# A two-layer mixer model on one core: the forgetting attention issued as one chain, its causal mask added by VectorE

## The chip, the cores and the metric

One core of one Trainium2 chip runs the whole program. The metric is device time in microseconds, the median of three runs. The engines are TensorE (PE, and PEld for its weight loads), VectorE (DVE), ScalarE (ACT), GpSimd (POOL) and SyncE (SP), which issues the weight transfers.

## The reference, cut to what matters

A first block of two layers (mixer and dense feed-forward, then mixer and mixture of experts) is followed by a second block. All 512 tokens are one sequence, the model width is 1024. Each mixer holds three branches, whose outputs are joined and multiplied by `w_out`: a gated delta rule, the forgetting attention (6 heads of 64) and a pooling branch. The attention is what changes:

```python
for i in range(T // FX_BLOCK):                 # blocks of 128 queries
    lo, hi = i * FX_BLOCK, (i + 1) * FX_BLOCK
    s = jnp.einsum('bhqd,bhkd->bhqk', q[:, :, lo:hi], k[:, :, :hi]).astype(F32) * scale
    s = s + c[:, :, lo:hi, None] - c[:, :, None, :hi]
    s = jnp.where(k_pos <= q_pos, s, -jnp.inf)
    p = jax.nn.softmax(s, axis=-1).astype(dt)
    outs.append(jnp.einsum('bhqk,bhkd->bhqd', p, v[:, :, :hi]))
```

There are 6 heads with 4 query blocks each, so 24 blocks per mixer; block i has 128(i+1) keys.

## The kernel before

`mixer` (it runs twice, for the layers 0 and 1) builds everything as Python generators, called fibers. `Fibers.run` is a planner: it keeps a virtual time, resumes the ready fiber with the best rank, adds a cost for each matmul, and so writes down one order of instructions for TensorE. `yield 3.0` means "not before 3 us from now", `yield on(...)` waits for an event that another fiber sets, and `yield "pf"` waits for a free PSUM bank of the kind `pf`, of which there are three. TensorE executes the written order as it stands (`manual_schedule`); each instruction still waits for its data by semaphores, and the planned waits themselves are not in the program. The other engines are ordered by the framework.

The fibers around the change, with their ranks (a lower one goes first):
- `scan` (0.2): the recurrence of the delta rule, eight chunks with six small matmuls or twelve at a time, banks `px`. When it ends, its result is normalised, transposed and gated (`dn`).
- `heads` (1): transposes queries and keys of a head into two `fF` tiles, through `pf` banks; a head waits for the last scores of the head two before it.
- `attend(k)` (2), three of them: fiber k handles the blocks k, k+3, k+6 and so on.
- `dense` (3): input projections, pooling and gate columns, then the output projection. This is in two halves of eight output tiles. The first needs the pooling branch and `fo[0]`, the attention's first two heads; the second waits for `fo[1]`, `fo[2]` (the last head pair) and `dn`. While a planned heat is low, `dense` and `attend` go ahead of the others.

A block u of `attend` (head h = u // 4, query block i = u % 4) waits for its head and for the scores of block u-1 to be issued, and takes a `pf` bank. TensorE multiplies queries by keys into it and then adds the mask with a second matmul, the identity times the mask, both in the single-pass format fp32r (`causal_r`, lines 1171 to 1177). VectorE takes the maximum (line 1087), ScalarE the exponential with its sum (1089), VectorE the reciprocal (1090) and the scaling (1091) into the tile `fP`. After a planned wait of 2.2 + 0.4(i+1) us TensorE transposes P back into the same bank and VectorE copies it out (1095); after another 0.7 + 0.12(i+1) us TensorE multiplies by the values, and ScalarE copies the result into `fo` (1101), after which the bank is free:

```python
yield 2.2 + 0.4 * (i + 1)
...
yield 0.7 + 0.12 * (i + 1)
...
act(fo[j][r, 128 * i:N], ps[r, 0:128], AF.Copy)
rel("pf", 0.5)
```

Of the kernel before, what the change touches and what calls it, by code (L numbers as in the profile page):

```python
# [11 lines left out]
F32R = mybir.dt.float32r  # L12
I32 = mybir.dt.int32
U32 = mybir.dt.uint32
AF = mybir.ActivationFunctionType
ALU = mybir.AluOpType
# [62 lines left out]
class Pack:  # L79
# [10 lines left out]
    def done(self):  # L90
        return np.ascontiguousarray(np.concatenate(self.cols, 1))
# [97 lines left out]
class Event:  # L189
    t = None  # L190


class Fibers:
# [17 lines left out]
    def rel(self, tag, lat=1.0):  # L211
        self.banks.setdefault(tag, []).append(self.t + lat)
# [72 lines left out]
class Net:  # L285
# [326 lines left out]
    def mixer(self, l, xd=None, moe=False):  # L612
        nc, A, L = self.nc, self.A, f"L{l}."
        F = self.F = self.pe.F = Fibers({"pm": 2, "pf": 3, "px": 3})
        on, done, rel = F.event, F.set, F.rel
# [15 lines left out]
        if xd is None:  # L631
            xd = self.spill_x()
        ident, bones, tri64 = self.const("ident"), self.const("bones"), self.const("tri64")
        g = {}
        cx = lambda a: a.rearrange("p (c x) -> p c x", c=8)
        tt, ts, stt, act = (nc.vector.tensor_tensor, nc.vector.tensor_scalar, nc.vector.scalar_tensor_tensor,
                            nc.scalar.activation)
# [12 lines left out]
        nc.vector.tensor_copy(fg[:, 1:2], self.p(L + "fk"))  # L650
        hon = self.sm("hon", 1)
        ts(hon, self.p(L + "on"), 0.5, None, op0=ALU.mult)
        idr, car = self.causal_r()
        tri_x = self.state_tri()
        kF, KB, Q, kT, qd = ([None] * 3 for _ in range(5))
        MQ = {}
# [2 lines left out]
        xt, fo, zs, py, dn = [None] * 3, [None] * 3, [], [], []  # L659
# [389 lines left out]
        fs = {}  # L1049

        def heads():
            yield on("U")
            for h in range(6):
                j, hh = h // 2, h % 2
                yield on("xt", j)
                if h > 1:
                    yield on("S", h - 2, 3)
                fs[h] = []
                for s in range(2):
                    yield "pf"  # L1060
                    ps = self.ps("pf")
                    for n in range(4):
                        self.pe.transpose(ps[0:65, 128 * n:128 * n + 128], xt[j][:, n, s, hh], ident)
                    f = self.t("fF", "g")
                    act(f[0:65], ps[0:65], AF.Copy, scale=fg[0:65, s:s + 1])
                    rel("pf", 0.9)
                    fs[h].append(f)
                done(0.9, "fs", h)

        def attend(k):  # L1070
            for u in range(k, 24, 3):
                h, i = u // 4, u % 4
                j, hh = h // 2, h % 2
                yield on("fs", h)
                if u:
                    yield on("S", (u - 1) // 4, (u - 1) % 4)
                if (hh, i) == (0, 0):
                    fo[j] = self.t("fo", "z")
                q, kk = fs[h]
                N = 128 * (i + 1)  # L1080
                yield "pf"
                ps = self.ps("pf")
                self.pe.matmul(ps[:, :N], q[0:65, 128 * i:N], kk[0:65, :N], start=True, stop=False)
                self.pe.matmul(ps[:, 128 * i:N], idr, car, start=False, stop=True)
                done(0.0, "S", h, i)
                nm = self.t("fnm", "fs", (128, 3), bufs=4)
                nc.vector.tensor_reduce(nm[:, 0:1], ps[:, :N], axis=AX, op=ALU.max, negate=True)
                P = self.t("fP", "q", (128, 2, T))[:, 0]
                act(P[:, :N], ps[:, :N], AF.Exp, bias=nm[:, 0:1], accum_out=nm[:, 1:2])
                nc.vector.reciprocal(nm[:, 2:3], nm[:, 1:2])  # L1090
                ts(P[:, :N], P[:, :N], nm[:, 2:3], None, op0=ALU.mult)
                yield 2.2 + 0.4 * (i + 1)
                for jj in range(i + 1):
                    self.pe.transpose(ps[:, 128 * jj:128 * jj + 128], P[:, 128 * jj:128 * jj + 128], ident)
                nc.vector.tensor_copy(P[:, :N], ps[:, :N])
                yield 0.7 + 0.12 * (i + 1)
                r = slice(64 * hh, 64 * hh + 64)
                for jj in range(i + 1):
                    self.pe.matmul(ps[r, 0:128], fv[:, jj, 64 * h:64 * h + 64],
                                   P[:, 128 * jj:128 * jj + 128], start=jj == 0, stop=jj == i)  # L1100
                act(fo[j][r, 128 * i:N], ps[r, 0:128], AF.Copy)
                rel("pf", 0.5)
                if (hh, i) == (1, 3):
                    done(0.5, "fo", j)

        for rank, gen in enumerate((rstd(), gates(), scan(), intra(), keys(), decay(), values())):
            F.add(gen, 0.1 * rank)
# [1 line left out]
            F.add(queries(j), 0.7)  # L1109
            F.add(qnorm(j), 0.8)  # L1110
        F.add(heads(), 1)
        for k in range(3):
            F.add(attend(k), 2)
        F.add(dense(), 3)
        if moe:
            F.add(self.dispatch(), 0.01)
# [50 lines left out]
        nc.gpsimd.tensor_scalar(y[:, 16:], s[:, 16:], pin, None, op0=ALU.mult)  # L1167
        nc.gpsimd.tensor_tensor(y, y, x, op=ALU.subtract)


    def causal_r(self):
        if not hasattr(self, "_cr"):
            t = self.M.tile([128, 2, 128], F32R, name="car", bufs=1)
            self.nc.vector.tensor_copy(t[:, 0], self.const("ident"))
            self.nc.vector.tensor_copy(t[:, 1], self.const("causal"))
            self._cr = (t[:, 0], t[:, 1])
        return self._cr

    def swiglu(self, f, pg, pu, R):
        nc = self.nc  # L1180
# [1195 lines left out]
```

## Time and profile before

| | us |
|---|---|
| median of 3 runs | 2715.37 (2712.01 to 2716.12) |
| profiled execution, its own time | 2711.52 |
| its span, first to last instruction | 2709.7 |
| TensorE busy in the span | 2582.4 (95%) |
| VectorE busy | 1578.1 (58%) |
| ScalarE busy | 1126.0 (42%) |
| mean granted TensorE clock | 0.977 |

The mixers' attention lies at 195.7 to 289.4 us and at 877.7 to 976.8 us of the span. The granted clock is a share of 2.4 GHz, so 0.50 is 1.2 GHz. In the rows an engine's busy time in a stretch can be subtracted from the length of the stretch to get its idle time. Rows of matmuls overlap, since they are pipelined; distances between starts tell what one costs in a stream.

### The profile page before, as it was taken

What the parts mean: (1) busy time and instruction counts of PE and PEld (TensorE: products, weight loads), DVE (VectorE), ACT (ScalarE), POOL (GpSimd) and SP (SyncE); (2) the same over time, 40 slices, a digit from 0 to 9 for tenths busy, and PEclk for the clock granted to TensorE, in tenths of its full rate; (3) what the DMA queues carried; (4) which work ended last, traced back from release to release, by engine and by line L of the source; (5) the groups of instructions that cost most, each with busy time, mean ns of one, the idle gap of its engine ahead of it and who ended that gap; (6) DMA issues with size and microseconds to landing.
All of it is one profiled execution on the core that took longest, in us unless ns stands there. A gap on an engine that the chain in (4) does not pass through costs nothing.

```text
span 2709.7 us, 44079 instructions
## 1 busy us (share of the span) xinstructions
PE 2582.4 (95%) x18168; PEld 2001.5 (74%) x18168; DVE 1578.1 (58%) x2269; ACT 1126.0 (42%) x1608; POOL 376.5 (14%) x295
## 2 busy tenths in 40 slices
PE   7999999999999999999999998899989999999997
PEld 6787788888778667777777776566666676788887
DVE  5856743434575655666766675566744644644445
ACT  4344432223434534555555555464323334433332
POOL 4332000000333301000000001143432000000000
PEclk9999999999999999999999999999999999999999
DMA  3111222222312226687777766413232522222221
GB/s 115 55 57 41 85 93 94 94 93 96 116 55 65 67 79 230 250 309 276 269 266 275 254 253 229 169 67 109 82 118 88 174 87 69 88 98 94 95 93 56
DMA packets 102610, 359.41 MB, mean 133 GB/s; under 512 B 12416, under 2 KB 17920, under 8 KB 102400
## 3 DMA queue, kind: packets, MB, share of 16 engines
q1 hardware_dynamic: 82656, 307.42, 33.1%
q0 software_dynamic: 7840, 26.22, 2.8%
q10 hardware_dynamic: 11904, 22.86, 2.3%
q8 instruction: 145, 2.38, 0.4%
q14 instruction: 65, 0.53, 0.1%
HBM read 331.28 MB, written 25.17 MB: 132 GB/s over the span
## 4 chain that ended last, share of the span: by engine, by line
PE 56%; DVE 7%; issue 3%; DMA 2%; ACT 2%; POOL 0%; ACTq 0%; DVEq 0%; POOLq 0%; SPq 0%
PE pm L278 34%; PE px L278 11%; PE pf L278 10%; PE px L282 1%; DVE ipr L477 1%; DVE cy L673 0%; DMA raw<-in_s_gu_dram 0%; DVE G L1583 0%; PE pf L282 0%; DVE wlo L398 0%; DMA ye<-y 0%; DVE Tl L478 0%; DMA yb<-ye,slot 0%; DMA ya<-ye,slot 0%; DVE wl L2029 0%
## 5 line engine op out<-in xcount | busy, mean ns | idle before, releaser
L396 ACT ACTIVATE whi<-raw 128x1024 fp32r<-128x1024 f32 (+5 forms) x304 | 297.6, 979 | 776.6 <-PE pm L278 519.5
L278 PE MATMUL pm<-xsh,whi 128*128 128x512 f32 x1280 | 530.7, 415 | 10.8 <-ACT xsh L371 5.0
L278 PE MATMUL pm<-xsl,whi 128*128 128x512 f32 x1280 | 511.5, 400 | 2.6 <-DVE xsl L372 2.6
L278 PE MATMUL pm<-xsh,wlo 128*128 128x512 f32 x1280 | 511.2, 399 | 2.7 <-POOL wlo L398 2.6
L2029 DVE TENSOR_TENSOR wl<-raw,wh 128x1536 fp32r<-128x1536 f32 (+1 forms) x224 | 341.4, 1528 | 190.2 <-PE pf L278 86.2
L2028 ACT ACTIVATE wh<-raw 128x1536 fp32r<-128x1536 f32 (+1 forms) x224 | 291.5, 1305 | 251.9 <-PE pf L278 127.7
L278 PEld LDWEIGHTS pm<-xsh,whi 128*128 128x128 f32 x1280 | 244.8, 191 | 87.9 <-issue 19.8
L278 PEld LDWEIGHTS pm<-xsl,whi 128*128 128x128 f32 x1280 | 244.8, 191 | 62.3 <-DVE xsl L372 6.1
L278 PEld LDWEIGHTS pm<-xsh,wlo 128*128 128x128 f32 x1280 | 243.9, 191 | 62.7 <-POOL wlo L398 5.0
L398 DVE TENSOR_TENSOR wlo<-raw,whi 128x1024 fp32r<-128x1024 f32 (+5 forms) x230 | 251.8, 1095 | 61.2 <-ACT whi L396 61.0
L398 POOL TENSOR_TENSOR wlo<-raw,whi 128x1024 fp32r<-128x1024 f32 x74 | 181.6, 2454 | 355.7 <-ACT whi L396 341.8
L278 PE MATMUL pm<-hidl,whi 128*128 128x512 f32 (+1 forms) x328 | 126.7, 386 | 0.0
L278 PE MATMUL pm<-hidh,wlo 128*128 128x512 f32 (+1 forms) x328 | 126.4, 385 | 0.0
L278 PE MATMUL pm<-hidh,whi 128*128 128x512 f32 (+1 forms) x328 | 125.9, 384 | 0.0
L278 PE MATMUL pf<-raw,xs 128*32 128x384 f32 x1024 | 102.5, 493 | 0.0
L278 PE MATMUL pm<-wh,xh 128*128 128x384 f32 x256 | 91.9, 370 | 8.0 <-ACT wh L2028 6.6
L1213 DVE TENSOR_TENSOR X<-X,pm 128x512 f32<-128x512 f32 x40 | 27.5, 687 | 120.2 <-PE pm L278 120.2
L278 PE MATMUL pm<-wl,xh 128*128 128x384 f32 x256 | 87.4, 342 | 2.9 <-DVE wl L2029 2.9
L278 PE MATMUL pm<-wh,xl 128*128 128x384 f32 x256 | 86.0, 336 | 0.0
L278 PE MATMUL pf<-wh,xl 128*128 128x384 f32 x256 | 85.8, 336 | 0.0
L278 PE MATMUL pf<-wl,xh 128*128 128x384 f32 x256 | 85.6, 335 | 0.0
L278 PE MATMUL pf<-wh,xh 128*128 128x384 f32 x256 | 84.4, 335 | 0.0
(625 smaller groups left out, 4805.2 us busy)
## 6 DMA issues: line engine op xcount, KB each, us to landing
raw<-in_s_gu_dram SPq DMA_DIRECT2D x128, 768.0 KB, 6.3
raw<-in_s_dn_dram SPq DMA_DIRECT2D x96, 512.0 KB, 4.0
raw<-in_f_gu_dram SPq DMA_DIRECT2D x44, 512.0 KB, 3.2
raw<-in_b_gu_dram SPq DMA_DIRECT2D x44, 512.0 KB, 3.2
raw<-in_b_wi_dram SPq DMA_DIRECT2D x38, 512.0 KB, 3.8
raw<-in_wq_dram SPq DMA_DIRECT2D x28, 512.0 KB, 3.5
raw<-in_f_dn_dram SPq DMA_DIRECT2D x16, 512.0 KB, 3.2
raw<-in_b_dn_dram SPq DMA_DIRECT2D x16, 512.0 KB, 3.2
```

The costliest lines, as they stand in the source:

```text
L278: return self.nc.tensor.matmul(o, l, r, **k)
L282: return self.nc.tensor.transpose(o, a, i)
L396: nc.scalar.activation(hi, raw, AF.Copy)
L398: (eng or nc.vector).tensor_tensor(lo, raw, hi.bitcast(F32), op=ALU.subtract)
L477: nc.vector.tensor_tensor(pr, A_, T_, op=ALU.mult)
L1213: nc.vector.tensor_tensor(self.X[m], self.X[m], ps, op=ALU.add)
L2028: self.wmark = act(hi, raw, AF.Copy)
L2029: tt(lo, raw, hi.bitcast(F32), op=ALU.subtract)
```

## The change

`attend` becomes one fiber with one loop over 26 steps. Step u issues the scores of block u, the values of block u-2 and the transposes of block u-1 together, with no planned wait between them, and one wait of 2.0 + 0.25(i+1) us at its end. The mask is added in PSUM by VectorE ahead of the maximum, and the fp32r copies of identity and mask are gone.

```diff
-        idr, car = self.causal_r()
...
-        def attend(k):
-            for u in range(k, 24, 3):
+        def attend():
+            blocks = {}
+            def scores(u):
                 h, i = u // 4, u % 4
-                yield on("fs", h)
-                if u:
-                    yield on("S", (u - 1) // 4, (u - 1) % 4)
...
-                yield "pf"
                 ps = self.ps("pf")
-                self.pe.matmul(ps[:, :N], q[0:65, 128 * i:N], kk[0:65, :N], start=True, stop=False)
-                self.pe.matmul(ps[:, 128 * i:N], idr, car, start=False, stop=True)
+                self.pe.matmul(ps[:, :N], q[0:65, 128 * i:N], kk[0:65, :N], start=True, stop=True)
                 done(0.0, "S", h, i)
                 nm = self.t("fnm", "fs", (128, 3), bufs=4)
+                tt(ps[:, 128 * i:N], ps[:, 128 * i:N], self.const("causal"), op=ALU.add)
                 nc.vector.tensor_reduce(nm[:, 0:1], ps[:, :N], axis=AX, op=ALU.max, negate=True)
...
-                yield 2.2 + 0.4 * (i + 1)
-                for jj in range(i + 1):
-                    self.pe.transpose(ps[:, 128 * jj:128 * jj + 128], P[:, 128 * jj:128 * jj + 128], ident)
-                nc.vector.tensor_copy(P[:, :N], ps[:, :N])
-                yield 0.7 + 0.12 * (i + 1)
+                blocks[u] = ps, P
+
+            def values_of(u):
+                ps, P = blocks.pop(u)
...
                 rel("pf", 0.5)
...
+            def turned(u):
+                ps, P = blocks[u]
+                N = 128 * (u % 4 + 1)
+                for j in range(0, N, 128):
+                    self.pe.transpose(ps[:, j:j + 128], P[:, j:j + 128], ident)
+                nc.vector.tensor_copy(P[:, :N], ps[:, :N])
+
+            for u in range(26):
+                if u < 24:
+                    yield on("fs", u // 4)
+                    yield "pf"
+                    scores(u)
+                if u > 1:
+                    values_of(u - 2)
+                if 0 < u < 25:
+                    turned(u - 1)
+                yield 2.0 + 0.25 * (u % 4 + 1) if u < 24 else 1.5
...
-        for k in range(3):
-            F.add(attend(k), 2)
+        F.add(attend(), 2)
```

## Rows read from the trace of the kernel before

**Rows 1.** The page: the span, and busy time of each engine.

```profile
span 2709.7 us, 44079 instructions
...
PE 2582.4 (95%) x18168; PEld 2001.5 (74%) x18168; DVE 1578.1 (58%) x2269; ACT 1126.0 (42%) x1608; POOL 376.5 (14%) x295
```

**Rows 2.** Table of stretches: length, busy us (instructions) by engine, granted clock, DMA share, GB/s.

```profile
195.70:302.60 106.90, 104.19 (x939) 77.84 (x938) 70.87 (x175) 49.44 (x125) 18.25 (x23) 0.98 0.13 42
289.40:302.60 13.20, 13.20 (x57) 10.66 (x58) 7.89 (x13) 4.15 (x8) 0.00 (x0) 1.00 0.33 96
...
877.70:990.10 112.40, 105.47 (x940) 78.08 (x939) 75.13 (x180) 54.42 (x137) 24.97 (x33) 0.97 0.20 63
...
976.80:990.10 13.30, 13.30 (x58) 10.79 (x59) 7.99 (x13) 4.15 (x8) 0.00 (x0) 1.00 0.34 96
```

**Rows 3.** TensorE in time order, first mixer: start, us, line, operation, x records.

```profile
226.59 0.65 PE L282 MATMUL pf<-cst,fP 128*128 128x128 f32 x4
227.08 0.39 PE L278 MATMUL pf<-fF 65*128 65x128 f32 x2
227.23 0.31 PE L278 MATMUL pf<-car 128*128 128x128 f32 x1
227.37 0.65 PE L278 MATMUL pf<-fF 65*128 65x256 f32 x2
...
228.20 0.39 PE L278 MATMUL pm<-xsl,whi 128*128 128x512 f32 x1
228.43 0.39 PE L278 MATMUL pm<-xsh,wlo 128*128 128x512 f32 x1
228.75 1.09 PE L278 MATMUL pf<-fP,fv 128*64 128x128 f32 x8
229.77 0.56 PE L278 MATMUL px<-Xc,Uf 64*64 64x64 f32 x12
```

**Rows 4.** TensorE's waits in both attentions: us in total, times, longest.

```profile
PE pf L278 <- ACT fo L1101: 1.1, 1, 1.1
PE px L278 <- ACT vn L994: 0.4, 1, 0.4
...
PE pf L278 <- ACT fo L1101: 2.2, 1, 2.2
PE pf L278 <- ACT fF L1065: 1.6, 1, 1.6
PE pf L278 <- DVE fP L1095: 0.8, 2, 0.6
PE pf L282 <- DVE fP L1091: 0.8, 1, 0.8
```

**Rows 5.** Stretches of 2 us, columns as in Rows 2: the clock behind stalls.

```profile
248.00:250.00 2.00, 0.97 (x3) 0.49 (x3) 2.00 (x4) 1.97 (x5) 0.00 (x0) 1.00 0.11 43
...
252.00:254.00 2.00, 2.00 (x7) 1.51 (x7) 0.88 (x3) 0.78 (x2) 0.00 (x0) 0.50 0.00 0
...
934.00:936.00 2.00, 0.00 (x0) 0.00 (x0) 1.97 (x6) 1.99 (x8) 0.77 (x2) 0.50 0.84 283
```

**Rows 6.** Softmax steps by tile (ns min/median/max), last: a PSUM addition (busy us, ns).

```profile
L1089 ACT ACTIVATE fP<-pf,fnm x48: 357/521/691, 198.0 to 970.8; 128x128 f32<-128x128 f32 x12, 128x256 f32<-128x256 f32 x12, 128x384 f32<-128x384 f32 x12, 128x512 f32<-128x512 f32 x12
L1089 ACT ACTIVATION_READ_ACCUMULATOR fP<-pf,fnm x48: 191/193/210, 198.3 to 971.3; 128x1 f32 x48
L1091 DVE TENSOR_SCALAR fP<-fP,fnm x48: 275/380/893, 199.3 to 972.9; 128x128 f32<-128x128 f32 x12, 128x256 f32<-128x256 f32 x12, 128x384 f32<-128x384 f32 x12, 128x512 f32<-128x512 f32 x12
L1095 DVE COPY fP<-pf x48: 269/481/685, 200.2 to 974.9; 128x128 f32<-128x128 f32 x12, 128x256 f32<-128x256 f32 x12, 128x384 f32<-128x384 f32 x12, 128x512 f32<-128x512 f32 x12
...
L1087 DVE TENSOR_REDUCE fnm<-pf x48: 278/484/692, 196.2 to 970.0; 128x1 f32<-128x128 f32 x12, 128x1 f32<-128x256 f32 x12, 128x1 f32<-128x384 f32 x12, 128x1 f32<-128x512 f32 x12
...
L1090 DVE RECIPROCAL fnm<-fnm x48: 144/156/164, 199.0 to 972.2; 128x1 f32<-128x1 f32 x48
...
L982 DVE TENSOR_TENSOR Xc<-px,nbe 128x192 f32<-128x192 f32 x7 | 2.5, 354 | 2.2 <-PE px L278 2.2
```

More of the change, by code (lines that the diff above doesn't have):

```diff
@@ L1068, in heads @@
                 done(0.9, "fs", h)
-        def attend(k):
-            for u in range(k, 24, 3):
+        def attend():
+            blocks = {}
+            def scores(u):
                 h, i = u // 4, u % 4
-                j, hh = h // 2, h % 2
-                yield on("fs", h)
-                if u:
-                    yield on("S", (u - 1) // 4, (u - 1) % 4)
-                if (hh, i) == (0, 0):
-                    fo[j] = self.t("fo", "z")
+                if u % 8 == 0:
+                    fo[h // 2] = self.t("fo", "z")
                 q, kk = fs[h]
                 N = 128 * (i + 1)
-                yield "pf"
                 ps = self.ps("pf")
-                self.pe.matmul(ps[:, :N], q[0:65, 128 * i:N], kk[0:65, :N], start=True, stop=False)
-                self.pe.matmul(ps[:, 128 * i:N], idr, car, start=False, stop=True)
+                self.pe.matmul(ps[:, :N], q[0:65, 128 * i:N], kk[0:65, :N], start=True, stop=True)
                 done(0.0, "S", h, i)
                 nm = self.t("fnm", "fs", (128, 3), bufs=4)
+                tt(ps[:, 128 * i:N], ps[:, 128 * i:N], self.const("causal"), op=ALU.add)
                 nc.vector.tensor_reduce(nm[:, 0:1], ps[:, :N], axis=AX, op=ALU.max, negate=True)
@@ L1091, in attend @@
                 ts(P[:, :N], P[:, :N], nm[:, 2:3], None, op0=ALU.mult)
-                yield 2.2 + 0.4 * (i + 1)
-                for jj in range(i + 1):
-                    self.pe.transpose(ps[:, 128 * jj:128 * jj + 128], P[:, 128 * jj:128 * jj + 128], ident)
-                nc.vector.tensor_copy(P[:, :N], ps[:, :N])
-                yield 0.7 + 0.12 * (i + 1)
-                r = slice(64 * hh, 64 * hh + 64)
+                blocks[u] = ps, P
+            def values_of(u):
+                h, i = u // 4, u % 4
+                ps, P = blocks.pop(u)
+                r = slice(64 * (h % 2), 64 * (h % 2) + 64)
                 for jj in range(i + 1):
@@ L1100, in attend @@
                                    P[:, 128 * jj:128 * jj + 128], start=jj == 0, stop=jj == i)
-                act(fo[j][r, 128 * i:N], ps[r, 0:128], AF.Copy)
+                act(fo[h // 2][r, 128 * i:128 * i + 128], ps[r, 0:128], AF.Copy)
                 rel("pf", 0.5)
-                if (hh, i) == (1, 3):
-                    done(0.5, "fo", j)
+                if u % 8 == 7:
+                    done(0.5, "fo", h // 2)
+            def turned(u):
[14 more added lines that the diff above has]
+                yield 2.0 + 0.25 * (u % 4 + 1) if u < 24 else 1.5
         for rank, gen in enumerate((rstd(), gates(), scan(), intra(), keys(), decay(), values())):
@@ L1168, in windows @@
         nc.gpsimd.tensor_tensor(y, y, x, op=ALU.subtract)
[L1171 to L1177, printed above, removed]
     def swiglu(self, f, pg, pu, R):
```

## The prediction, made before the result was known

> **What bounds the kernel now.** I read the page first, then a table of the stretches in which the attention of the two mixers runs, then the instructions of TensorE in order of time there, then what TensorE waited for, then the durations of the softmax steps. The page says that TensorE is the bound of the whole run: busy for 2582.4 of 2709.7 us [rows 1]. The change touches only two stretches. The first mixer's attention begins at 195.7 us, and its output projection has used up everything that does not need the last heads at 302.6; in the second mixer these points lie at 877.7 and 990.1 [rows 2]. In these stretches TensorE is idle for 106.90 - 104.19 = 2.7 us and 112.40 - 105.47 = 6.9 us. The mean granted clock is 0.98 and 0.97, so that up to 0.02 x 106.9 = 2.1 us and 0.03 x 112.4 = 3.4 us are lost to the lower level, 1.2 GHz. Take both away and each stretch holds 102.1 us of TensorE work at 2.4 GHz: the two agree to 0.1 us, as they should with the same list of instructions. So the stretch is TensorE work plus stalls, and the change can win only by removing work or stalls.
>
> One more pair of rows matters. From 289.4 (976.8), where the last block of attention has ended, to the end of the stretch TensorE is busy for 13.2 of 13.2 us (13.3 of 13.3) [rows 2]. This is projection work that needs only the first two heads. It covers the last block's softmax and the split of its result. Attention has so far a slack of 13 us.
>
> **Part 1: the mask leaves TensorE.** 48 matmuls (24 blocks, two mixers) of 128x128 against the identity go. Their rows are 0.3 us and more long, but matmuls overlap, so I take distances between starts. From the mask's start to the next start it is 0.14 us at the shortest [rows 3]; a matmul of 512 columns in the same number format follows its neighbour by 0.23 us, so 128 columns are 0.06 us. Between 48 x 0.06 = 2.8 and 48 x 0.14 = 6.7 us; I take 0.07, near the lower end, because the longer distance can hold the end of the scores' own stream: -3.4 us, 1.7 in each stretch. The Trainium skill (Perfetto Trace Analysis, Identifying the Most-Contended Engine) speaks against counting this: matmul busy time is no measure of how full TensorE is, weight-load time is. By that the 77.84 us of weight loads in 106.9 [rows 2] leave a quarter of it free and the term would be 0, the total 3.4 us higher; the trace agrees with the warning, since rows overlap, but the 0.23 us from start to start leaves no hole to fill.
>
> **Part 2: the mask comes to VectorE.** 48 additions of 128x128 from and to PSUM are not in the trace. The nearest rows are the evacuation of a 128x128 tile (0.27 us at least) and an addition of 128x192 with one operand in PSUM, 0.354 us [rows 6]; I take 0.29. That is 24 x 0.29 = 7.0 us on VectorE in each stretch, where it was busy for 70.87 of 106.9 us. It hides as long as blocks have slack. What is queued behind it on VectorE is the next scan step and the weight split, which TensorE waits for. Between 0 and 3 us in all; +1. The block's own latency from scores to probabilities becomes 0.29 + 0.48 (maximum) + 0.52 (exponential) + 0.19 (its sum) + 0.16 + 0.38 = 2.0 us by medians [rows 6]. The two casts at the start fall away with `causal_r`; they ran while the constants landed, 0.
>
> **Part 3: three interleaved chains become one.** This moves the most, in both directions.
>
> What it gives. Block u's transposes now stand a whole step behind its scores, its values another step behind that, and a PSUM bank is asked for a step after its eviction was issued instead of half a microsecond. The stalls of before are of just this kind: TensorE waited for the eviction `fo` (1.1 us in the first mixer, 2.2 in the second), for `fF` (1.6), for P's copy and scaling (0.8, 0.8) [rows 4]. Behind them the clock fell: 0.50 at 252 to 254 us after a stretch with 0.97 of 2 us busy, and 0.50 at 934 to 936, where nothing ran [rows 5]. Together there are 2.7 + 6.9 us idle and up to 2.1 + 3.4 us of clock, 15.1 us. Not all goes. The wait for `vn` is the scan's, and in the second mixer VectorE and ScalarE were both solid at 934 to 936 (1.97 and 1.99 of 2 us), so a backlog of some microseconds meets a slack of about two. Between 3 and 13 us; I take 60%, -9.
>
> What it costs. The order of TensorE is written by a planner, and the new chain waits 2.0 + 0.25(i+1) us after every step before the next may be issued. Over 24 blocks that is 24 x 2.0 + 0.25 x 60 + 1.5 = 64.5 us, one wait after another, where three chains used to wait side by side. The chain's own matmuls, from [rows 3]: per 128 columns of keys 0.23 us scores (0.29 less the mask), 0.49/4 = 0.12 transposes, 1.02/4 = 0.255 values, 0.61 x 60 = 36.5 us. The sum is 101.0 us against 102.1 - 1.7 = 100.4 us of all work that TensorE has there. So even if every step were picked up at once, the last block would be issued only when the covering work is gone; and it isn't picked up at once, for half a dense triple (0.35 us) is under way at the mean, more while the scan has the right of way: 24 x 0.35 = 8.4 us at least. So 9 us of planned waiting, 9/2.6 = 3.5 steps, have nothing beside them; I take 4, between 0 and 6. TensorE doesn't sit out planned waits, it follows the order as the data allow. An uncovered step then goes at VectorE's pace: 0.29 + 0.48 + 0.16 + 0.38 + 0.48 (copy) = 1.8 us against 1.5 us of matmuls, or 2.5 if VectorE also waits in order for the exponential (0.52 + 0.19). Lost per step 0.3 to 1.0, taken 0.5. After the last scores nothing stands between the block's softmax (2.4 to 2.9 us for the widest, with the longest maximum and exponential), its copy (0.68), its values and the split of `fo`, except the neighbours' transposes and values: some 3.5 us idle, 3 to 4. Per mixer 4 x 0.5 + 3.5 = 5.5 us, between 3 and 10: +11 in all (6 to 20). Such a thin stretch drops the clock as at 248 to 254; two microseconds lost each time, or none: +2 (0 to 5). Late next is thus the second half of the output projection, which waits for the last `fo`.
>
> `heads` keeps its rank and its two banks' worth of transposes and gets a free bank sooner; 0. No DMA queue is moved; the projection weights are fetched by the same stream, 0.
>
> **The sum.** -3.4 + 1 - 9 + 11 + 2 = +1.6 us on the profiled execution of 2711.5 us, whose span is 2709.7. The median of the runs is 2715.4, 3.9 us above it; carried over to that, 2717 us. First mixer: -1.7 - 2.9 + 6.5 + 0.5 = +2.4; second: -1.7 - 6.2 + 6.5 + 0.5 = -0.9.
>
> **The rivals.**
> Faster: the single chain removes nearly all stalls (-13) and the covering work lasts to the last block (+6, clock 0): -3.4 + 1 - 13 + 6 = -9.4, 2706 us. For it: nearly every wait in [rows 4] is one that an extra step of distance covers. Against it: 101.0 against 100.4 us leaves the cover no room.
> Slower: VectorE in the uncovered steps. If it works them in order, one block after another, a step costs 2.5 us; with six steps uncovered and the clock down behind them the tails cost 16 + 4 us: -3.4 + 1 - 9 + 20 = +8.6, 2724 us. It decides from four uncovered steps on at 2.5 us. For it: 7 us more on VectorE; the clock fell behind the stalls of before. Against it: the durations allow 1.8.
> Nothing from the mask (weight loads are what counts): +1.6 + 3.4 = +5.0, 2720 us, still inside the next bound.
>
> **How the numbers follow.** A measurement can tell 0.2%, 5.4 us, from no change. Forecast and the mask rival, within 5.4 us: 0.45 (0.38 and 0.07). Faster: 0.25. Slower: 0.30, a little more, since the tail follows from the written waits while the share of stalls that goes is a judgement. The likeliest case alone spans 2712 to 2721. For 8 in 10 the range takes in the two rivals' middles with a little beyond: 2705 to 2728.
>
> **What would show it.** Right: rows of the mask matmul gone and an addition of about 0.29 us before each maximum; the waits for `fo` and `fF` at 247 to 250 and 929 to 936 shorter; the last values within a microsecond or two of the second half of the projection, with TensorE waiting for P's copy, its scaling and the split of `fo` there, and a fall of the clock around 295 and 970. Wrong: projection work still standing behind the last values; or stalls as before in the middle; or the scan stretched by VectorE.

## The result, and the profile after

The kernel after takes 2737.68 us, the median of 6 runs (2733.73 to 2739.79); the kernel before took 2715.74 beside it (6 runs, 2710.59 to 2719.66). The ratio is 1.0077, with a 95% interval of 1.0065 to 1.009: 21 us slower. Forecast were 2717, between 2705 and 2728. The direction of the slower rival came, at more than twice its size.

The page of the kernel after, to hold against [rows 1]:

```profile
span 2735.4 us, 44016 instructions
...
PE 2600.8 (95%) x18120; PEld 2003.6 (73%) x18120; DVE 1594.9 (58%) x2315; ACT 1126.3 (41%) x1608; POOL 376.3 (14%) x295
```

TensorE has 48 instructions fewer and is busy for 18.4 us more. VectorE is busy for 16.8 us more; 48 x 0.30 = 14.4 of it are the new additions:

```profile
L1084 DVE TENSOR_TENSOR pf<-pf,cst x48: 282/300/300, 193.0 to 1003.3; 128x128 f32<-128x128 f32 x48
```

The stretches that answer to [rows 2], columns as there. In each mixer the first row begins with the first scores and ends where the covering work is used up; the second goes on to the first matmul of the output projection's second half:

```profile
192.40:282.50 90.10, 86.44 (x823) 62.98 (x821) 63.27 (x157) 41.39 (x98) 18.08 (x22) 1.00 0.16 50
282.50:310.90 28.40, 22.78 (x94) 14.27 (x92) 15.52 (x44) 8.22 (x27) 0.31 (x1) 0.73 0.08 23
...
886.00:981.40 95.40, 89.08 (x824) 64.52 (x821) 68.01 (x161) 46.66 (x110) 25.39 (x33) 0.96 0.22 70
981.40:1011.90 30.50, 25.56 (x94) 15.36 (x92) 15.45 (x45) 8.25 (x27) 0.00 (x0) 0.62 0.10 37
```

The second row of each pair is new. I call it the tail. Before, attention ended with 13 us of projection still to do; now the scores of block 16 come just behind the last covering matmul, and blocks 17 to 23 follow with nothing beside them. TensorE in time order there (start, us, line, operation):

```profile
282.05 0.39 PE L278 MATMUL pm<-foh,wlo 128*128 128x512 f32 x1
282.28 0.38 PE L278 MATMUL pf<-fF 65*128 65x128 f32 x2
```

TensorE is idle in the tail for 28.40 - 22.78 = 5.6 us and 4.9 us, and the mean clock is 0.73 and 0.62 there: 0.27 x 28.4 = 7.7 us and 0.38 x 30.5 = 11.6 us go to the lower level.

What TensorE waited for (us in total, times, longest), first in the covered part of the first mixer, then in its tail, then in the covered part of the second mixer:

```profile
PE pf L282 <- DVE fnm L1088: 1.8, 1, 1.8
PE px L278 <- DVE Xc L982: 0.8, 1, 0.8
...
PE pf L282 <- DVE fP L1089: 3.3, 3, 1.7
PE pf L278 <- DVE fP L1109: 2.2, 4, 0.9
...
PE pf L282 <- DVE fP L1089: 4.9, 2, 3.9
PE px L278 <- DVE Xc L982: 1.2, 2, 0.8
```

The waits for `fo` of [rows 4] are gone, as meant, but for 0.4 us in the first mixer. In their place transposes wait for the probabilities, at the same spot (246.4 and 942.2 us). So the idle time of the covered parts is 90.10 - 86.44 = 3.7 and 95.40 - 89.08 = 6.3 us, against 2.7 and 6.9 in all of the stretch before.

**Where the 25.7 us between the two spans went.** From here on I count from the first scores to the end of the whole output projection, so that every kernel below does the same work in it, and sum both mixers. Idle is the length less TensorE's busy time; clock is 1 less the granted clock, summed over pieces of 2 us; the rest is what is left, about TensorE's work at the full clock. Before: 283.3 us = 9.6 idle + 5.1 clock + 268.6. After: 311.3 = 20.5 + 25.6 + 265.2. So 10.9 us more idle, 20.5 more at the lower clock, 3.4 less rest, together +28.0. Ahead of the first attention 3.3 us are won, between the mixers 0.9; behind the second 1.8 are lost: 25.6. The front gain is not the change's: ahead of the first scores TensorE has the same 1945 matmuls in the same order in before, after and e3 below, and e3 begins at 195.4 us, as before does (195.7), where after begins at 192.4.

The rest falls by 3.4 us, which is what was forecast for the mask; how far one such number can be trusted, the next table shows.

### The profile page after: what moved, and what is told of

It is laid out like the page before. It is cut to its first block, busy times and chain, and to the rows that moved or that the text cites. A ratio compares the mean times of both kernels' runs of the same rounds, so it can differ in the third digit from the quotient of the medians.

```text
span 2735.4 us, 44016 instructions
## 1 busy us (share of the span) xinstructions
PE 2600.8 (95%) x18120; PEld 2003.6 (73%) x18120; DVE 1594.9 (58%) x2315; ACT 1126.3 (41%) x1608; POOL 376.3 (14%) x295
## 4 chain that ended last, share of the span: by engine, by line
PE 57%; DVE 7%; issue 2%; DMA 2%; ACT 2%; POOL 0%; ACTq 0%; DVEq 0%; POOLq 0%; SPq 0%
PE pm L278 34%; PE px L278 11%; PE pf L278 10%; PE px L282 1%; DVE ipr L477 1%; PE pf L282 1%; DVE cy L672 0%; DVE G L1590 0%; DVE wlo L398 0%; ACT whi L396 0%; DMA yb<-ye,slot 0%; DVE Tl L478 0%; DMA ye<-y 0%; DVE rk L1595 0%; DVE xx L1500 0%
## 5 line engine op out<-in xcount | busy, mean ns | idle before, releaser
L278 PE MATMUL pf<-wl,xh 128*128 128x384 f32 x256 | 85.8, 336 | 0.0
L278 PE MATMUL pf<-wh,xh 128*128 128x384 f32 x256 | 84.6, 336 | 0.0
```

The lines of the kernel that those rows point to most:

```text
L278: return self.nc.tensor.matmul(o, l, r, **k)
```

## The experiments

One table for all; ratios are to the kernel before on the same chip, the four columns on the right are from the profiled execution, in us, as just defined.

| run | median | ratio, 95% interval | length | idle | clock | rest |
|---|---|---|---|---|---|---|
| before | 2715.7 to 2717.1 | 1 | 283.3 | 9.6 | 5.1 | 268.6 |
| after | 2737.7 | 1.0077 (1.0065 to 1.009) | 311.3 | 20.5 | 25.6 | 265.2 |
| e1 mask only | 2713.6 | 0.9989 (0.9978 to 1.0) | 284.9 | 17.0 | 3.4 | 264.4 |
| e2 chain only | 2721.4 | 1.0026 (1.0015 to 1.0037) | 293.4 | 14.5 | 5.1 | 273.7 |
| e3 short waits | 2723.2 | 1.003 (1.0019 to 1.004) | 294.9 | 17.5 | 6.8 | 270.6 |
| e4 warm tail | 2732.7 | 1.0067 (1.0049 to 1.0085) | 305.2 | 15.4 | 5.1 | 284.6 |
| e5 middle waits | 2724.6 | 1.0035 (1.002 to 1.005) | 297.7 | 18.8 | 10.2 | 268.6 |
| e6 dn first | 2731.5 | 1.0069 (1.0045 to 1.0092) | 295.4 | 20.2 | 8.5 | 266.7 |
| e7 late mask | 2723.0 | 1.0022 (1.0008 to 1.0036) | 303.9 | 16.6 | 18.8 | 268.5 |
| e8 heads in px | 2724.9 | 1.0033 (1.0013 to 1.0052) | 296.9 | 19.8 | 8.5 | 268.7 |
| e9 mask, longer wait | 2707.95 | 0.9967 (0.9954 to 0.998) | 282.2 | 13.7 | 3.4 | 265.0 |
| e10 before, longer wait | 2712.2 | 0.9983 (0.9973 to 0.9993) | 277.2 | 8.1 | 3.4 | 265.7 |
| e11 short waits, mask on TensorE | 2712.0 | 0.9982 (0.9972 to 0.9991) | 282.4 | 9.1 | 0.0 | 273.3 |
| e12 cheap warm tail | 2736.4 | 1.0058 (1.004 to 1.0076) | 319.4 | 15.4 | 30.7 | 273.4 |

Each row of the four columns is one execution, and executions of one kernel scatter: those of before lie between 2710.5 and 2724.6 us. The profiled executions of e7 and e12 are the slowest of their kernels, those of e6, e9, e10 and e11 the fastest. Before and e10 have the same list of matmuls, and their rest still differs by 2.9 us. So a difference of about 3 us in one column shows little by itself; the 20 us of the clock stand far above that.

### The two parts apart: e1 and e2

e1 is the kernel before with

```diff
-                self.pe.matmul(ps[:, :N], q[0:65, 128 * i:N], kk[0:65, :N], start=True, stop=False)
-                self.pe.matmul(ps[:, 128 * i:N], idr, car, start=False, stop=True)
+                self.pe.matmul(ps[:, :N], q[0:65, 128 * i:N], kk[0:65, :N], start=True, stop=True)
...
+                tt(ps[:, 128 * i:N], ps[:, 128 * i:N], self.const("causal"), op=ALU.add)
```

> The kernel before with its three chains, with one part of the change alone: the mask is added by VectorE and the masking matmul is gone. Theory A (the single chain and its uncovered tail carry the whole loss): the mask is harmless here, 2711 to 2717 us. Rival B (the loss is VectorE's: 24 additions per mixer lengthen each step's latency and put the scan behind): above 2720 us, up to 2728.

e2 is the kernel after with these lines the other way round.

> The kernel after with the mask put back as a matmul on TensorE, so the single chain alone. Theory A: as slow as the kernel after or a little slower, 2738 to 2742 us (48 masking matmuls more, 3.4 us). Rival B: the loss was the mask's, 2725 us or less.

The mask alone gives -3.0 us by the ratio (-6 to 0, hardly to be told from no change), the chain alone +7 (4 to 10). For the first theory A held. For the second it fell: the chain by itself is only a third of the loss. Rival B's time came there (2721.4), but by e1 the mask alone is not the loss either. The sum of the parts is +4, the whole is +21, so 17 us belong to neither but to both together. The table says where: e2's clock column is as before, 5.1, after's 25.6. If the changes of e1 and e2 simply added up, the columns would be 21.9 idle, 3.4 clock and 269.5 rest; after has 20.5, 25.6 and 265.2. What the two parts make together is lost clock and no idle time. The tails of e2 are there as well, just as long in blocks (columns as above):

```profile
283.70:307.30 23.60, 20.32 (x103) 13.95 (x101) 13.95 (x36) 8.51 (x27) 0.31 (x1) 0.86 0.10 28
...
975.70:997.00 21.30, 17.68 (x104) 11.79 (x102) 13.77 (x37) 8.64 (x27) 0.00 (x0) 1.00 0.16 54
```

The second ran at full clock and took 21.3 us, where the kernel after needs 30.5. Idle in it: 3.6 us against 4.9.

### Is it the mask in the tail? e7

```diff
+                late = u >= 16
...
+                if late:
+                    self.pe.matmul(ps[:, 128 * i:N], idr, car, start=False, stop=True)
...
+                if not late:
+                    tt(ps[:, 128 * i:N], ps[:, 128 * i:N], self.const("causal"), op=ALU.add)
```

> The kernel after with the mask by VectorE in blocks 0 to 15 and by TensorE's matmul, as before, in blocks 16 to 23, so in the uncovered steps only. The single chain with all masks on TensorE ran 2721 us, with all on VectorE 2738. Theory C (the 16 us between them lie in the uncovered tail: the addition lengthens each step's way through VectorE, TensorE stands longer and its clock falls to 1.2 GHz): 2718 to 2724 us. Rival D (VectorE's additions cost in the covered part too): 2729 us or more.

2723.0 us, as theory C had it, and not to be told from e2. Sixteen of 24 additions may stay on VectorE at no cost that shows; the eight of the uncovered blocks carry the difference. A kernel with an addition in each tail step has 0.30 us more on the way from scores to probabilities, and less for TensorE to do meanwhile (0.07 us by the forecast's price).

The single runs of e7 reach from 2717.0 to 2731.8, and their mean clock from 0.979 to 0.973. The profiled one is the slowest, and its second tail shows why:

```profile
282.30:306.20 23.90, 20.42 (x103) 13.72 (x101) 13.87 (x36) 8.60 (x27) 0.31 (x1) 0.86 0.10 28
...
974.50:1004.10 29.60, 26.49 (x104) 17.73 (x102) 14.07 (x37) 8.64 (x27) 0.00 (x0) 0.62 0.12 39
```

The same tail as e2's, 104 matmul records and 3.1 us idle, at 0.62 instead of 1.00, and 8 us longer. With the mask on TensorE the clock in the tail is thus open from run to run; the kernel after lost it in each run (mean clock 0.968 to 0.970).

### The clock by itself: e4 and e12

```diff
+            def warm(n):
+                px = self.ps("px")
+                for _ in range(n):
+                    nc.tensor.matmul(px[:, 0:128], ident, ident, start=True, stop=True)
...
+                if u == 25:
+                    warm(6)
...
+                if 17 <= u < 25:
+                    warm(6 if u == 24 else 3)
```

> The kernel after with 27 + 12 matmuls of 128 x 128 on the identity, read by nobody, put into the uncovered tail of each mixer, three ahead of each group of transposes from block 17 on and six ahead of each of the last groups, where TensorE stands idle for VectorE or ScalarE. They fill 0.37 us of a gap of 0.4 to 1.7 us. Theory C (about 8.6 us per mixer of the loss is the tail at 1.2 GHz, since TensorE falls to the lower level after gaps): the tail runs nearer to 2.4 GHz and is 20 to 24 us instead of 28 to 30, in all 2721 to 2729 us. Rival D (the tail is bound by the latency of a step through VectorE and ScalarE, and the low clock costs nothing): 2735 us or more.

e12 has `idr, car` in place of `ident, ident`.

> The kernel after with the same unread matmuls in the uncovered tails as in the run with the warm tail, 39 in each mixer, but in the single-pass format of 0.07 us instead of the fp32 one. The earlier run showed that clock loss in the tails went from 20 us to nothing and that its 39 matmuls cost 9.2 us per mixer, 0.235 each. Theory C (the clock of the tail is the larger part of the loss, and little work in the gaps holds it up): 5 us of unread matmuls and 20 us of clock won, 2720 to 2726 us. Rival D (such short matmuls don't hold the clock): 2736 us or more.

The tails of e4, then of e12:

```profile
285.70:312.10 26.40, 23.88 (x161) 17.97 (x159) 15.63 (x44) 8.39 (x27) 0.31 (x1) 1.00 0.09 26
981.90:1008.30 26.40, 23.89 (x161) 17.95 (x159) 15.66 (x45) 8.37 (x27) 0.00 (x0) 1.00 0.13 45
```

```profile
282.70:317.00 34.30, 31.95 (x128) 22.54 (x126) 15.81 (x44) 8.47 (x27) 0.31 (x1) 0.60 0.07 20
985.00:1018.60 33.60, 31.24 (x128) 22.09 (x126) 15.95 (x45) 8.41 (x27) 0.00 (x0) 0.61 0.10 35
```

In e4 the clock stays at 1.00 through both tails and these become shorter, 26.4 us instead of 28.4 and 30.5, though each holds 39 matmuls more. So the clock was a loss of its own and not a mere sign of waiting. The gain in time is small, 5 us by the medians and 3 by the ratios, whose intervals overlap, and the time lies between the two theories. That is my price's fault: I had taken 0.12 us for an fp32 matmul of 128 columns, the price of a transpose; by the rest column it is (284.6 - 265.2)/78 = 0.25 us, what the values cost in the forecast. With the short format the 39 matmuls do not hold the clock in the profiled execution: 0.60 and 0.61, and the median, 2736.4, is theory D's. But this execution is the slowest of four; the fastest took 2727.1 us at a mean clock of 0.978, where e4's four have 0.976 to 0.978. So here too the clock is open from run to run. I have found no way to hold it that pays.

### More cover: e3, e5, e6, e8

e3, and e5 with 0.9 + 0.12 in place of 0.6 + 0.1:

```diff
-                yield 2.0 + 0.25 * (u % 4 + 1) if u < 24 else 1.5
+                yield 0.6 + 0.1 * (u % 4 + 1) if u < 24 else 0.5
```

> The kernel after with one line changed: the due time of the chain's next step is 0.6 + 0.1 per 128 keys instead of 2.0 + 0.25, so the steps are issued closer together. Theory A (the loss is the seven steps of a mixer that come after all covering work is used up): the last scores are issued while the dense matmuls still run, the tail is gone, 2703 to 2716 us. Rival B (three matmul groups in one lump, waiting in TensorE's order for VectorE and ScalarE, cost by themselves): the stalls move into the covered part, 2727 us or more.

> The kernel after with the chain's wait set between its own and that of the run with 0.6 + 0.1: 0.9 + 0.12 us per 128 keys. That run had its last values 7.4 us before the dense work ended, and 24 x 0.3 + 60 x 0.02 = 8.4 us more of written waits just use that up. Theory A (the seven uncovered steps are the loss, and the stalls of the shorter wait come from transposes that follow their scores too soon): no tail and shorter stalls, 2712 to 2720 us. Rival B (three matmul groups in a lump cost by themselves, whatever the wait): 2724 us or more.

In both, the last values start before the dense work ends: no tail. Of the loss of 21 us, 13 go in e3 and 11 in e5 by the ratios. Neither theory is met by e3, B by e5: what remains is stalls in the covered part. e3 waits 4.7 us for line 1089 in the first mixer (e11, which differs by the mask alone, has no such row):

```profile
PE pf L282 <- DVE fP L1089: 4.7, 4, 2.6
PE px L278 <- DVE S L1010: 1.5, 2, 1.3
```

e6 moves the delta rule's result into the first half of the projection:

```diff
...
-        specs += [(self.flat(A[f"wo_a{l}"][m]), (3, 128)) for m in range(8)]
-        specs += [(self.flat(A[f"wo_b{l}"][m]), (5, 128)) for m in range(8)]
+        specs += [(self.flat(A[f"wo_a{l}"][m]), (6, 128)) for m in range(8)]
+        specs += [(self.flat(A[f"wo_b{l}"][m]), (2, 128)) for m in range(8)]
...
+            yield on("dn")
+            cat += dn
...
-                    yield on("dn")
-                    cat += dn
```

> The kernel after, its chain and waits untouched, but the delta rule's result `dn` is multiplied in the first half of the output projection instead of the second: 8 x 3 x 3 matmuls of 512 columns at 0.235 us, 16.9 us of covering work more ahead of the last heads, the total the same. Theory A (what costs is the end of the covering work before the last block): a covered step takes 4.5 us of which 1.5 are its own, so 5 to 6 of the 7 uncovered steps are covered now; the tail shrinks from 28.5 and 30.6 us to some 10, in all 2714 to 2722 us. Rival B (the steps are slow, covered or not): 2732 us or more.

In the profile theory A's mechanism is there: the covering work of the first mixer lasts to the scores of block 23 (311.9 us), its tail is 8.4 us (about 9.5 in the second mixer), and the clock column falls from 25.6 to 8.5. In time it is a miss: 2731.5, with four runs between 2724.5 and 2737.4 and the profiled one the fastest. Idle stays at 20.2, since stalls in the covered part come up (4.9 us at 945, for the probabilities). The spread I can't explain.

e8 changes the bank that `heads` takes and gives back, in three lines:

```diff
-                    yield "pf"
-                    ps = self.ps("pf")
+                    yield "px"
+                    ps = self.ps("px")
...
-                    rel("pf", 0.9)
+                    rel("px", 0.9)
```

> The kernel after with the transposes of `heads` in banks of the kind px instead of pf, so that they no longer take a bank that the chain waits for. In the kernel after the steps behind a head's transposes (blocks 4, 8, 12, 16) come 6.3 to 8.7 us after the one before, where others come after about 5. Theory E (the banks that heads takes delay the chain by some 10 us per mixer): two of the seven uncovered steps become covered, some 4 us less in each mixer, 2727 to 2732 us. Rival F (the delay is the data's and the scan's, not the bank's): 2735 us or more.

Both theories are surpassed: 2724.9, 12 us less than after by the ratios. Block 16 is issued 84.6 us after block 0 instead of 89.8 (second mixer: 85.8 instead of 95.1), the blocks behind the cover are five instead of eight, and the tails are 18.6 us:

```profile
291.50:310.10 18.60, 13.93 (x67) 8.57 (x65) 11.07 (x30) 5.91 (x19) 0.31 (x1) 0.86 0.10 32
981.40:1000.00 18.60, 13.93 (x67) 8.57 (x65) 11.06 (x31) 5.89 (x19) 0.00 (x0) 0.85 0.10 29
```

The banks that `heads` takes, which I had put at 0, cost the chain 5 and 9 us of issue time.

### Versions that beat the kernel before: e9, e10, e11

e9 is e1, e10 is the kernel before, each with

```diff
-                yield 2.2 + 0.4 * (i + 1)
+                yield 2.6 + 0.45 * (i + 1)
```

> The three chains with the mask added by VectorE, and the planned wait between a block's scores and its transposes 2.6 + 0.45 us per 128 keys instead of 2.2 + 0.4: the 0.29 us that the addition takes are given back. Theory A (in the run with the mask alone TensorE waits 7 and 10 us, 4.8 and 6.3 of it for VectorE or ScalarE ahead of transposes that come too early; the mask's 3.4 us are won in full once these go): 2704 to 2710 us. Rival B (VectorE is behind there by more than a wait can give): 2712 us or more.

> The kernel before with the same longer wait and nothing else, as a control. Theory A (there TensorE waits for evictions and free banks, hardly for transposes): 2712 to 2719 us, no difference. Rival B (a gain of the run above comes from the wait and not from the mask): 2710 us or less.

e11 is e2 with e3's waits.

> The single chain with waits of 0.6 + 0.1 us, which had no uncovered tail and ran 2723 us, now with the mask by TensorE. Theory A (its stalls come from the longer way through VectorE): the stalls ahead of transposes (1.3 and 2.6 us in each mixer) shrink by more than the mask's 3.4 us of TensorE: 2714 to 2720 us. Rival B (the lump, not the mask: transposes one step behind their scores wait for VectorE in any case): 2722 us or more.

e9 is the best, 2707.95 us or 9 us less than before (5 to 12), by theory A: the idle time that the mask had brought (17.0 in e1) falls to 13.7. But the control, forecast as no difference, gives 5 us (2 to 7) without a change of the mask, so at most part of it is the mask's; the intervals of the two overlap, and their profiled spans (2704.1 and 2703.1) do not tell them apart.

e11 shows that the single chain is no loss in itself. With waits so short that it ends within the cover, and the mask on TensorE, it beats the kernel before by 5 us (2 to 8), beyond what theory A expected; in its profiled execution no time at the lower clock is left in either mixer:

```profile
194.00:330.10 136.10, 132.42 (x1060) 99.50 (x1059) 93.51 (x202) 63.16 (x146) 18.11 (x23) 1.00 0.18 56
876.00:1022.30 146.30, 140.87 (x1073) 99.60 (x1072) 93.03 (x203) 65.17 (x152) 34.24 (x39) 1.00 0.25 77
```

Against e11, e3 with the mask on VectorE has 8.4 us more idle, 6.8 more at the lower clock and 2.7 less rest, and takes 13 us more by the ratios. In three chains the idle time rises nearly as much (7.4 in e1), but the clock does not fall with it: the chain, whose transposes stand only one step behind their scores, is the place where 0.30 us on VectorE hurt.

## Why the prediction was wrong, step by step

**The mask's matmuls, -3.4: right as far as it can be seen.** In the four pairs that differ by the mask alone the rest column falls by 4.2 (before to e1), 0.7 (e10 to e9), 8.5 (e2 to after) and 2.7 (e11 to e3), 4.0 at the mean, and it moves by 2.9 without any change of the work. By the Trainium skill's rule on weight loads (Perfetto Trace Analysis, Identifying the Most-Contended Engine) it would have been 0. Four falls of four speak against that here, though only the 8.5 stands clearly above that scatter.

**The mask on VectorE, +1 (0 to 3): too small.** The addition's size (0.30 against 0.29 us) and its place were right. But TensorE idles longer with it in each of the four pairs: by 7.4, 5.6, 6.0 and 8.4 us, in the order above. In three chains the balance of both terms still came near in time, -2.4 by forecast and -3.0 (-6 to 0) in e1, in part by luck: e1's columns add up to 1.6 us more, not less. In the single chain it did not. What I did not ask was who is late by 0.30 us once nothing covers the step: in the tail it is TensorE, eight times per mixer, and with it the clock (e7).

**The stalls, -9: wrong.** Idle time in the covered parts is 3.7 + 6.3 = 10.0 us, before it was 9.6 in the stretch. The -9 took in the clock as well: 9.6 + 5.1 = 14.7 us by the table before, and 10.0 + 0.04 x 95.4 = 13.8 in the covered parts of after, so that about 1 us was won. I had read [rows 4] as waits for banks and evictions that one more step of distance covers. They were a backlog of VectorE and ScalarE, and this is still there. Before, ahead of the 2.2 us wait for `fo` that ends at 936.15 (start, us, line, operation):

```profile
932.54 1.92 DVE L1035 TENSOR_TENSOR oT<-oT,oss 128x512 f32<-128x512 f32 x3
```

```profile
930.65 1.28 ACT L1030 ACT_TABLE_LOAD   x1
...
932.76 1.28 ACT L1089 ACT_TABLE_LOAD   x1
```

The values that this eviction copies were there at 931.2; on ScalarE it came after the loads and what stood between and behind them, at 935.84. VectorE and ScalarE of the kernel after ahead of the 3.9 us wait that ends at 942.22:

```profile
935.03 0.28 DVE L1085 TENSOR_REDUCE fnm<-pf 128x1 f32<-128x128 f32 x1
...
938.86 0.41 DVE L1085 TENSOR_REDUCE fnm<-pf 128x1 f32<-128x256 f32 x1
939.20 2.48 DVE L1034 TENSOR_TENSOR oT<-oT,oss 128x512 f32<-128x512 f32 x3
941.60 0.21 DVE L1088 RECIPROCAL fnm<-fnm 128x1 f32<-128x1 f32 x2
941.79 0.55 DVE L1089 TENSOR_SCALAR fP<-fP,fnm 128x128 f32<-128x128 f32 x2
```

```profile
936.43 0.91 ACT L1957 ACTIVATE msk<-mem,mg 128x256 fp32r<-128x256 f32 x2 [1.09 <-DMA mem<-in_mem_dram]
937.24 0.61 ACT L1962 ACTIVATE msq<-mem 128x512 f32<-128x512 f32 x1
937.88 1.28 ACT L1087 ACT_TABLE_LOAD   x1
939.17 0.37 ACT L1087 ACTIVATE fP<-pf,fnm 128x128 f32<-128x128 f32 x1
```

The block's maximum is there at 935.31, its exponential starts at 939.17. In between ScalarE waits 1.09 us for a transfer, works on `msk` and `msq`, which belong to a later part of the model, and loads a table; so the load is a third of the delay. The reciprocal then waits for three normalisations of the delta rule's result. The Trainium skill (ScalarE activation tables: per-element evaluation and per-set limits, What a function is on this engine) says that functions of different sets are one load of 1283 ns apart; the 1.28 us here agree. The forecast had written "a backlog of some microseconds meets a slack of about two", and then taken 60% all the same.

**The number of uncovered blocks, 4 (0 to 6): wrong, it was 8.** The sum of written waits and own work, 4.2 us per step, was right as a lower bound, but the pickup was too small. From block 0 to block 16 the chain needs 89.84/16 = 5.6 us per step, so 1.4 instead of 0.35 come on top. Shown is one part of that, the banks of `heads` (e8: 5.2 us in 16 steps, 0.3 per step). Others are argued: the planner counts 512 columns as 512/2400 = 0.213 us where they take 0.23 [rows 3], so that each written microsecond lasts longer, and the scan goes first.

**The tail's idle time, +11: right by luck.** Measured 5.6 + 4.9 = 10.5 us. Twice as many blocks were uncovered, but each lost less: in the first mixer some 2.7 us in eight steps, where 0.5 each was taken, and 2.9 behind the last scores instead of 3.5. The way of one wait, TensorE, VectorE and ScalarE in the tail of the first mixer:

```profile
284.84 1.09 PE L278 MATMUL pf<-fP,fv 128*64 128x128 f32 x8 [0.31 <-DVE fP L1109]
287.58 0.30 PE L282 MATMUL pf<-cst,fP 128*128 128x128 f32 x1 [1.65 <-DVE fP L1089]
```

```profile
284.09 0.69 DVE L1109 COPY fP<-pf 128x512 f32<-128x512 f32 x1 [0.71 <-PE pf L282]
284.70 0.28 DVE L1085 TENSOR_REDUCE fnm<-pf 128x1 f32<-128x128 f32 x1
...
286.75 0.16 DVE L1088 RECIPROCAL fnm<-fnm 128x1 f32<-128x1 f32 x1 [0.84 <-ACT fP L1087]
286.83 0.41 DVE L1085 TENSOR_REDUCE fnm<-pf 128x1 f32<-128x256 f32 x1
287.15 0.28 DVE L1089 TENSOR_SCALAR fP<-fP,fnm 128x128 f32<-128x128 f32 x1
```

```profile
285.96 0.27 ACT L1099 ACTIVATE fo<-pf 64x128 f32<-64x128 f32 x1 [2.19 <-PE pf L278]
286.26 0.37 ACT L1087 ACTIVATE fP<-pf,fnm 128x128 f32<-128x128 f32 x1
```

Block 16's exponential could have run at 285.0, its maximum was there. On ScalarE it stands behind the eviction `fo` of block 15, which waits for the values at 284.84, which wait for the copy at 284.09. So block 16 hangs on block 15 through the order of VectorE and ScalarE. This is the in-order work of the slower rival, which I had held for less likely: from scores to scores the tails' steps took 2.7 and 2.9 us at the mean, for the most part at the lower clock, nearer to its 2.5 than to 1.8.

**The clock, +2 (0 to 5): wrong, the largest error.** It is +20.5 us over all; 7.7 + 11.6 = 19.3 us are lost in the tails. I had priced a fall as a passing event of two microseconds behind one stall, as in [rows 5]. In the tail a fall lasts: from 290 to 298 us and again from 306 to 312, and in the second mixer from 990 to the end of the tail, all at 0.50 by pieces of 2 us. TensorE may be busy throughout at the lower level:

```profile
296.00:298.00 2.00, 2.00 (x7) 1.35 (x8) 0.90 (x3) 0.58 (x3) 0.00 (x0) 0.50 0.00 0
...
306.00:308.00 2.00, 2.00 (x10) 1.52 (x9) 0.00 (x0) 0.27 (x1) 0.00 (x0) 0.50 0.00 0
...
994.00:996.00 2.00, 2.00 (x8) 1.25 (x6) 0.52 (x1) 0.62 (x3) 0.00 (x0) 0.50 0.00 0
```

The slower rival (2724) had the direction, the place and the pace, and six uncovered steps; short was its 4 us for the clock. In the sum, with the chain's own +7 of e2 against the +4 that its terms made, and the mask's -3.0 against -2.4, each part alone would have been forecast within 3 us, though not by its terms: in e2 the clock is unchanged, idle is up by 4.9 us and the rest by 5.1, which I can't explain. The 17 us of their meeting are in the clock, which I had at +2.

**What would show it.** The signs that the forecast named for itself came: the addition ahead of each maximum, the waits for `fo` and `fF` shorter or gone, TensorE waiting in both tails for P's copy and scaling, and the clock falling there, in the second mixer at 988 us instead of 970. The last values stand 1.9 us ahead of the second half (309.04 and 310.94). One of its signs of being wrong came too: stalls as before in the middle, 10.0 us. So where the loss would arise was read rightly; the stalls that were to go, the number of uncovered blocks and the price of the clock were not.

## What to carry to other kernels

When work is moved off the cover's end, price the uncovered stretch at the lower clock as well as at the full one, and take the dearer as a case: here the clock cost twice what the gaps did. Two edits that cost little or nothing alone can meet in such a stretch; ask of each what it adds to the latency of a step that nothing covers. A planned wait in a hand-written order is a rate: check that the last step is still issued while covering work is left, with every other user of the same banks counted, and tune it with the change (0.6 + 0.1 instead of 2.0 + 0.25 us, with the mask left on TensorE, makes the same chain 5 us faster than the kernel before).

## What the runs showed of the hardware

The clock of a thin stretch is not settled by the list of instructions. The same tail, the same 104 matmul records, ran at 1.00 in 21.3 us (e2, second mixer) and at 0.62 in 29.6 us (e7), with 3.6 and 3.1 us idle. The kernel after lost it with no gap above 1.7 us and TensorE busy for 80 and 84% of the tails. The Trainium skill (TensorE: Matmul & The Clock Gate, HAM oscillation — how this bites in real kernels) describes a loop whose waits for DMA bring the clock down again and again, each of them longer than any gap here; this trace shows a fall without such a gap. What decides between the two outcomes here stays open.

What filler holds the clock is open too. With 39 fp32 matmuls of 128 columns per tail, 0.25 us each, it stayed at 1.00 in e4's profiled execution. With as many in the single-pass format it fell to 0.60 and 0.61 in e12's, but the mean clocks of e12's four runs reach from 0.970 to 0.978, so it did not fall as far in each.
